# Ten quads instead of eight, a second lane for the state-space constants, the sink as a score column, and another division of PSUM

## The chip, the core and the metric

The kernel runs on one core of a Trainium2 chip. The core has five engines with queues of their own: TensorE (PE, its weight loads shown as PEld), VectorE (DVE), ScalarE (ACT), GpSimd (POOL) and SyncE (SP, here only a queue that issues DMAs). Work is measured in device microseconds for one execution; lower is better. A profile of one execution shows every instruction with its engine, its line of the kernel and its tile.

## What is computed

One step of a hybrid decoder layer for two groups of tokens that share all weights: 16 meta tokens and 512 prompt tokens, and 8 sample tokens with caches. Of the reference, what matters here:

```python
xn = rmsnorm(x, norm_gain)
h = einsum('btd,de->bte', xn, w_in)              # 2048 -> 8704
q, k, v, z_a, u, z_s, g_a, g_s = split(h)
q, k = rope(rmsnorm(q, gq)), rope(rmsnorm(k, gk))
# sliding window of 128 with 16 meta keys and a sink per head
m = maximum(max(s), sink); p = exp(s - m)
w = p / (sum(p) + exp(sink - m)); o = w @ v
# state space: 64 groups of 64 complex states, one linear recurrence over time
lam_bar = exp(lam * dt); b_bar = (lam_bar - 1) / lam * b
h_t = lam_bar * h_{t-1} + b_bar u_t;  y = real(c h) + d u
y = gelu(y); y = y * sigmoid(y @ w_glu + b_glu)
out = x + (sigmoid(g_a) * ((o * silu(z_a)) @ w_attn_out) + sigmoid(g_s) * ((y * silu(z_s)) @ w_ssm_out)) @ w_out
```

Everything is float32. The large products run as three matmuls of a faster float32 format each: both operands are split into a high and a low part (hi·hi, lo·hi, hi·lo).

## The kernel before, in words

The 536 tokens lie in two halves of 268 columns. A weight **unit** is 1024 rows by 128 columns; `Stream.piece` (L825) loads it (`raw`, a DMA on SP's queue), ACT casts the high part (`whi`, L829) and DVE subtracts for the low part (`wlo`, L830). A **block** of 128 output columns, `mm` (L938), takes two units: 16 k-tiles, three products, two halves. `xblock` (L969) makes a block of the gates and z parts and `evac` (L977) writes it to DRAM (`gD`).

A **quad** (`quad`, L1124, with `Quads`, L847) makes two blocks at once by seven products of half size each instead of eight (Strassen's scheme): `product` (L1117) issues 8 x 3 matmuls for each, from weights that are partly sums made by DVE (L887) and split like the others (L888, L889), and from sums of the inputs (`tau`, L1168). `NA` (L768) plain blocks run first while the tau are made, then `NQ` quads. Eight more quads do the last matrix, `w_out`.

The order of PE: five blocks beside the loading of x; four plain blocks; eight quads; then 27 blocks in the order of `ORDER1` (L771): 7 x blocks, 12 heads blocks (q, k, v; raw to `rawD`), 8 u blocks; then the remaining x blocks up to 47 (L1336); one block that is split around the reading of the state-space output (L1341); 8 blocks of `w_glu` with one unit each (L1363), 16 of `w_ssm_out` (L1379), 16 of `w_attn_out` on A (L1398) and the last quads.

Beside this runs **background** work, written as generators in the two lanes of `Background` (L777). After every 24 main matmuls `mm` calls `bg.step` with half a budget (`BUDGET`, `BUDGET2` and so on, L762 and 763); a generator yields its cost in us or `None`, which ends its lane's turn; the credit left over is cut to 0.5. In lane 0 come first the tau, then `ssm_prep` (L67), then for each u block `ssm`: `ssm_consts` (L235), the constants of that block, and `ssm_block` (L326), the recurrence: U is read back from DRAM, B·U on PE (L357), two scans on DVE (L386), C·H on PE (L406, L408), gelu. Then `attention` (L1268): ten loads of constants, `keys` (L498), `values` (L524, transposes L540), and for each of four key heads `queries` (L547) and four `blocks` (L634): `scores` (L561, 8 matmuls into two PSUM buffers, read by ACT L576 and DVE L578), `softmax` (L581), `turn` (transposes, L604) and `weigh` (L623). After the first key head `sample` (L668) starts in lane 1: it streams the sample's cache through DVE with DMAs on POOL's queue, and ends at L757. When both lanes are empty, `attended` (L1307) multiplies the result by the gate, read back by POOL (`zr`, L1322), and splits it into A (L1304, L1305). In attention each background instruction is ordered behind the last weight split on DVE.

The framework orders each engine's instructions by a timeline that it simulates when the program is built (`schedule_with_timeline_sim=True`, L1595), by priority and by when inputs and buffers come free there; on the chip each engine then works strictly in that order and waits where an input is later than planned. Weights and evacuations have a higher priority (`HIGH`).

PSUM has eight banks. Four belong to `mm` (two buffers of two banks) and four to `aux`, which serves all background products and the heads' sums: two buffers of two banks, one name.

## Time and profile before

| | |
|---|---|
| median of 3 runs | 1306.85 us (1305.33 to 1308.04) |
| profiled execution, its own time | 1305.66 us |
| its span | 1303.8 us |
| PE, DVE, ACT, POOL busy | 1287.2, 970.7, 529.2, 51.6 us |
| quads (115 to 271 us): PE, DVE, ACT busy of 156 us | 156.00, 122.60, 74.12 |
| state-space blocks (367 to 690): of 323 us | 322.50, 254.90, 82.43 |
| attention, first half (690 to 860): of 170 us | 164.23, 113.74, 89.78 |
| attention, second half (860 to 1047): of 187 us | 186.72, 134.13, 94.33 |
| mean granted clock of PE | 0.997 |

Busy times are sums over instructions of an engine; a matmul's shown duration overlaps the next one's, so the distance between matmuls is the measure of PE's pace and not their mean length. In a row of groups stand line, engine, operation, tiles, shape and count, then busy time and mean ns, then idle time before them and what ended it. In a row of waits stand the waiter, what it waited for, the total, how often, and the longest.

### The profile page before, as it was taken

How to read it: one execution, taken by the hardware profiler on the slowest of the kernel's cores; microseconds unless marked ns; L12 is line 12 of the kernel's file. 1: busy time of each engine (PE TensorE's matmuls, PEld its weight loads, DVE VectorE, ACT ScalarE, POOL GpSimd, SP SyncE). 2: the span in 40 equal slices, each digit the busy share in tenths (PEclk: the TensorE clock that was granted, in tenths of full speed). 3: DMA queues.
4: the chain of work that ended last, by engine and by line, in shares of the span. 5: the costliest groups of instructions: out<-in, count | busy, mean ns of one | idle time of the engine just before them, and what ended most of it. 6: DMA issues, size and time to landing. Idle time of an engine off the chain costs nothing.

```text
span 1303.8 us, 26285 instructions
## 1 busy us (share of the span) xinstructions
PE 1287.2 (99%) x10525; PEld 1250.8 (96%) x10525; DVE 970.7 (74%) x1723; ACT 529.2 (41%) x988; POOL 51.6 (4%) x115
## 2 busy tenths in 40 slices
PE   9999999999999999999999899999999999999998
PEld 8999999999999999999999899989998999999998
DVE  7586887768799788777963865878766677888775
ACT  8553444432222222222222567556544333344442
POOL 0000000000000000000004002111001100000000
PEclk9999999999999999999999899999999999999999
DMA  9554344243466554455447752666465865554441
GB/s 293 191 171 147 106 140 161 74 151 116 142 176 179 146 144 147 136 151 139 127 145 181 208 156 86 179 234 198 149 208 185 282 218 179 179 176 150 146 146 50
DMA packets 114010, 211.64 MB, mean 162 GB/s; under 512 B 29356, under 2 KB 54044, under 8 KB 113856
## 3 DMA queue, kind: packets, MB, share of 16 engines
q1 hardware_dynamic: 109216, 196.07, 48.3%
q0 software_dynamic: 4672, 13.89, 3.7%
q8 instruction: 83, 1.36, 0.4%
q14 instruction: 39, 0.32, 0.1%
HBM read 178.87 MB, written 33.13 MB: 163 GB/s over the span
## 4 chain that ended last, share of the span: by engine, by line
PE 82%; DMA 7%; issue 4%; DVE 2%; ACT 2%; SPq 1%; POOL 1%; POOLq 0%; DVEq 0%; ACTq 0%
PE mm L949 49%; PE pr L1120 23%; PE aux L628 2%; PE aux L1120 1%; DMA zr<-gD 1%; PE aux L357 1%; PE aux L408 1%; PE aux L949 1%; PE mm L1034 1%; DMA t<-gD 1%; PE aux L406 1%; PE aux L1100 1%; DVE wlo L830 1%; DMA uD<-uf 1%; DMA k_kg<-in_kg 1%
## 5 line engine op out<-in xcount | busy, mean ns | idle before, releaser
L949 PE MATMUL mm<-xh,whi 128*128 128x260 f32 (+1 forms) x1504 | 312.4, 288 | 0.0
L949 PE MATMUL mm<-xh,wlo 128*128 128x260 f32 (+1 forms) x1504 | 308.0, 285 | 0.0
L949 PE MATMUL mm<-xl,whi 128*128 128x260 f32 (+1 forms) x1504 | 306.7, 285 | 0.0
L829 ACT CAST whi<-raw 128x1024 fp32r<-128x1024 f32 (+3 forms) x156 | 152.2, 982 | 306.7 <-PE mm L949 234.3
L949 PEld LDWEIGHTS mm<-xh,whi 128*128 128x128 f32 x1504 | 233.9, 189 | 7.7 <-issue 7.6
L949 PEld LDWEIGHTS mm<-xl,whi 128*128 128x128 f32 x1504 | 234.6, 189 | 0.8 <-issue 0.8
L949 PEld LDWEIGHTS mm<-xh,wlo 128*128 128x128 f32 x1504 | 233.6, 189 | 1.6 <-issue 1.6
L830 DVE TENSOR_TENSOR wlo<-raw,whi 128x1024 fp32r<-128x1024 f32 (+3 forms) x156 | 176.5, 1137 | 65.7 <-ACT whi L829 64.1
L889 DVE TENSOR_TENSOR wlo<-raw,whi 128x1024 fp32r<-128x1024 f32 x112 | 134.5, 1222 | 48.7 <-ACT whi L888 48.2
L888 ACT CAST whi<-raw 128x1024 fp32r<-128x1024 f32 x112 | 115.6, 1049 | 120.5 <-PE pr L1120 40.9
L1120 PE MATMUL pr<-cb,whi 128*128 128x260 f32 x848 | 153.1, 283 | 2.4 <-ACT whi L888 2.4
L1120 PEld LDWEIGHTS pr<-cb,whi 128*128 128x128 f32 x848 | 130.8, 188 | 2.8 <-ACT whi L888 2.8
L949 PE MATMUL mm<-Y,whi 128*128 128x260 f32 x768 | 129.1, 286 | 0.3 <-DVE Y L1305 0.2
L1120 PE MATMUL pr<-cb,wlo 128*128 128x260 f32 x424 | 118.9, 283 | 0.0
L949 PEld LDWEIGHTS mm<-Y,whi 128*128 128x128 f32 x768 | 106.7, 188 | 6.4 <-issue 5.8
L1120 PE MATMUL pr<-tau,whi 128*128 128x260 f32 x480 | 86.6, 283 | 0.0
L949 PE MATMUL mm<-A,whi 128*128 128x260 f32 x512 | 82.5, 283 | 0.0
L1120 PEld LDWEIGHTS pr<-cb,wlo 128*128 128x128 f32 x424 | 79.6, 188 | 0.0
L949 PE MATMUL mm<-Y,wlo 128*128 128x260 f32 x384 | 79.2, 286 | 0.0
L887 DVE TENSOR_TENSOR raw<-raw 128x1024 f32<-128x1024 f32 x64 | 78.2, 1222 | 1.3
L1120 PEld LDWEIGHTS pr<-tau,whi 128*128 128x128 f32 x480 | 73.7, 188 | 0.0
L949 PEld LDWEIGHTS mm<-A,whi 128*128 128x128 f32 x512 | 70.3, 188 | 0.3 <-DVE A L1305 0.3
(415 smaller groups left out, 2026.3 us busy)
## 6 DMA issues: line engine op xcount, KB each, us to landing
raw<-in_w SPq DMA_DIRECT2D x202, 512.0 KB, 3.8
gD<-z SPq DMA_DIRECT2D x48, 260.0 KB, 2.7
t<-gD SPq DMA_DIRECT2D x32, 260.0 KB, 2.8
cache<-in_vc POOLq DMA_DIRECT2D x16, 286.0 KB, 3.5
cache<-in_kc POOLq DMA_DIRECT2D x15, 288.0 KB, 3.5
xr<-in_x SPq DMA_DIRECT2D x16, 268.0 KB, 5.6
xg<-in_x SPq DMA_DIRECT2D x8, 536.0 KB, 5.4
sD<-z SPq DMA_DIRECT2D x16, 260.0 KB, 2.7
```

The source lines that it names most:

```text
L357: nc.tensor.matmul(bu[:, i, 140 * e:140 * e + 140], lhsT=D["B"][:, i, 2 * h + e], rhs=U[:, 2 * h + e, 8:16 + NC], start=True, stop=True)
L406: nc.tensor.matmul(o, lhsT=R["T"][:, a], rhs=U[:, a, 0:140], start=True, stop=False)
L408: nc.tensor.matmul(o, lhsT=D["CL"][:, a, i, 1:5], rhs=H[:, a, i, 0:140], start=False, stop=(i == 1))
L628: nc.tensor.matmul(pv[64 * e:64 * e + 64, 0, 0:256], lhsT=V, rhs=pr[:, e::2], start=(i == 0), stop=(i == len(parts) - 1))
L829: nc.scalar.copy(out=hi, in_=raw)
L830: self.dve = nc.vector.tensor_tensor(out=lo, in0=raw, in1=hi.bitcast(F32), op=ALU.subtract).ins
L887: nc.vector.tensor_tensor(out=o, in0=o, in1=i, op=ALU.add)
L888: nc.scalar.copy(out=hi, in_=t)
L889: nc.vector.tensor_tensor(out=lo, in0=t, in1=hi.bitcast(F32), op=ALU.subtract)
L949: m = nc.tensor.matmul(ps[:, c, 0:W], lhsT=wt[:, k], rhs=xo(kt, c), start=f, stop=l)
L1034: nc.tensor.matmul(ps[:, c, 0:260], lhsT=wt[:, kt % 8], rhs=xo[:, kt, c, 8:CH], start=f, stop=l)
L1120: m = nc.tensor.matmul(bank, lhsT=wt[:, p], rhs=x(p, e), start=first and f and p == 0, stop=l and p == 7, skip_group_check=not first and l ...
```

## The change

`NQ` goes from 8 to 10, so 20 of the x blocks are made by quads and 11 in place of 15 are left for the end of the loop; `XORDER` puts the blocks 32 to 39 ahead of 24 to 31. In `ssm_prep` all small normalisations but one go. The constants of the eight state-space blocks become one generator in lane 1, with double buffers, up to two sets ahead; their products with a per-partition factor go from DVE to ACT (`times`). The U of a block is loaded as soon as its buffer is free. `Background` keeps up to 3 (later 2) of credit, serves the lanes in turn until attention and lane 0 first from then on; budgets and some costs are new. In attention the constants come with one load, the values' and keys' loads are issued first, the values come before the keys, the sample starts at once, the second half of each key tile is copied by a DMA on POOL's queue, and the sink becomes a 145th score column, written by POOL, so that maximum and sum include it. The four background banks become one pair (`aux`) and two single banks (`tr`, `wg`); during the state-space blocks these are held as fixed regions. The `w_glu` blocks' tanh goes to SBUF instead of in place in PSUM. The diff, cut to its core:

```diff
     for n in ("z2", "z4"):
         nz = tmp.tile([P, 2, 32], F32, name=n)
         cmul(nc, tmp, nz, z, z[:, 0], z[:, 1], (32,), "c32_")
-        norm(nz, (32,), "n32")
         z = nz
     zs = yield from powers(T6, z, 6, "za")
     Z = tmp.tile([P, 2, 32], F32, name="Z")
     cmul(nc, tmp, Z, zs[2], zs[1][:, 0], zs[1][:, 1], (32,), "c32_")
-    norm(Z, (32,), "n32")
...
     cmul(nc, tmp, c, Zs[3], Zs[1][:, 0], Zs[1][:, 1], (32,), "c32_")
     cmul(nc, tmp, c2, c, Z[:, 0], Z[:, 1], (32,), "c32_")
+    norm(c2, (32,), "n32")
...
+def ssm_consts(nc, pool, dram, R, D, ub, a_bT, a_bN, a_cT, e32, d_skip, later, free):
...
+    bN = pool.tile([P, 4, 2, 32], F32, name="bN", bufs=1)
+    nc.sync.dma_start(out=bN, in_=a_bN[:, ps])
+    c = pool.tile([P, 4, 2, 32], F32, name="c", bufs=1)
...
+    yield 0.0
+    yield None
...
+
+    def times(dst, src, x):
+        nc.scalar.activation(out=dst, in_=src, func=AF.Copy, scale=x)
+
+    for a in range(4):
+        q = slice(4 * ub + a, 4 * ub + a + 1)
+        for i, k in enumerate(("Fre", "nFre")):
+            times(s1[:, a, i], bN[:, a, i], R[k][:, q])
+        times(s2[:, a], bN[:, a], R["nFim"][:, q])
+    yield 0.0
+    yield None
+    for r, t in ((0, t1), (1, t2)):
+        for k in range(4):
+            for a in range(4):
+                times(t[:, a, :, k], c[:, a], R["lamp"][:, r, k, 4 * ub + a:4 * ub + a + 1])
+            if k % 2:
+                yield 0.0
+                yield None
+    while not free():
+        yield None
+    B = pool.tile([P, 2, 512], F32, name="B")
     nc.sync.dma_start(out=B, in_=a_bT[ub])
...
-    v.tensor_tensor(out=t1, in0=B, in1=bc(f4[:, 0], 1, 2), op=ALU.mult)
-    v.tensor_tensor(out=t2, in0=B, in1=bc(f4[:, 1], 1, 2), op=ALU.mult)
-    yield 2.4
...
-            v.tensor_tensor(out=t[:, :, i], in0=bc(c[:, :, i], 2, 4), in1=bc(lp, 3, 32), op=ALU.mult)
-        yield 1.4
+    yield 3.8
+    v.tensor_tensor(out=bb[:, :, 0], in0=s1[:, :, 0], in1=s2[:, :, 1], op=ALU.add)
+    v.tensor_tensor(out=bb[:, :, 1], in0=s1[:, :, 1], in1=s2[:, :, 0], op=ALU.add)
+    yield 0.6
...
-    s1 = pool.tile([P, 4, 2, 32], F32, name="s1", bufs=1)
-    s2 = pool.tile([P, 4, 2, 32], F32, name="s2", bufs=1)
-    bb = pool.tile([P, 4, 2, 32], F32, name="bb", bufs=1)
...
+    kp = R["kp"]
+    with later():
+        for a in range(4):
+            for i in range(2):
...
-    d0 = pool.tile([P, 8, L], F32, name="d0", bufs=1)
+    d0 = R["d0"][ub % 2]
...
     tab = D["tab"]
...
+    with later():
+        for h in range(2):
+            for e in range(2):
+                for i in range(2):
+                    nc.tensor.matmul(place(h, i, e), lhsT=D["B"][:, i, 2 * h + e], rhs=U[:, 2 * h + e, 8:16 + NC],
+                                     start=True, stop=True)
+    yield 0.0
+    yield None
...
     with later():
-        y = psum.tile([P, 2, 512], F32, name="aux")
...
-                for part in (slice(0, 64), slice(64, 128)):
-                    for dst, src in zip(tm(KH, part), (*T, M)):
-                        nc.scalar.copy(out=dst, in_=src)
-                for part in (slice(0, 64), slice(64, 128)):
-                    for dst, src, hi in zip(tm(KL, part), (*T, M), tm(KH, own)):
-                        v.tensor_tensor(out=dst, in0=src, in1=hi.bitcast(F32), op=ALU.subtract)
-                    yield 0.8
+                for dst, src in zip(tm(KH, own), (*T, M)):
+                    nc.scalar.copy(out=dst, in_=src)
+                for dst, src, hi in zip(tm(KL, own), (*T, M), tm(KH, own)):
+                    v.tensor_tensor(out=dst, in0=src, in1=hi.bitcast(F32), op=ALU.subtract)
+                other = slice(64 - 64 * h, 128 - 64 * h)
+                for K in (KH, KL):
+                    nc.gpsimd.dma_start(out=K[other], in_=K[own])
+                yield 1.0
...
-        sb = pool.tile([P, 2, CH], F32, name="sb")
+        sb = pool.tile([P, 2, CH], F32, name="sv")
...
-        vb = pool.tile([P, 4, P], F32, name="vb", tag="rb")
+        vb = pool.tile([P, 4, P], F32, name="vb", tag=("po", "pp")[e], bufs=1)
...
-            ps = self.psum.tile([P, 2, 512], F32, name="aux")
+            ps, pm = (self.psum.tile([P, 512], F32, name=n) for n in ("tr", "wg"))
             for b in range(4):
-                nc.tensor.transpose(out=ps[:, 0, 128 * b:128 * b + 128], in_=vb[:, b], identity=self.C["idn"])
...
-        S = pool.tile([P, 4, 144], F32, name="S")
+        S = pool.tile([P, 4, 145], F32, name="S")
+        nc.gpsimd.tensor_copy(out=S[:, :, 144], in_=C["sink"][:, 4 * kv:4 * kv + 4])
         for j in range(2):
...
-        sk = C["sink"][:, 4 * kv:4 * kv + 4]
         v.tensor_reduce(out=m, in_=S, axis=AX.X, op=ALU.max)
-        v.scalar_tensor_tensor(out=m, in0=m, scalar=0.125, in1=sk, op0=ALU.mult, op1=ALU.max)
-        nm = pool.tile([P, 4], F32, name="nm")
-        v.tensor_scalar(out=nm, in0=m, scalar1=-1.0, scalar2=None, op0=ALU.mult)
+        v.tensor_scalar(out=m, in0=m, scalar1=-0.125, scalar2=None, op0=ALU.mult)
         den = pool.tile([P, 4], F32, name="den")
         for r in range(4):
-            nc.scalar.activation(out=S[:, r], in_=S[:, r], func=AF.Exp, bias=nm[:, r:r + 1], scale=0.125,
+            nc.scalar.activation(out=S[:, r], in_=S[:, r], func=AF.Exp, bias=m[:, r:r + 1], scale=0.125,
                                  accum_out=den[:, r:r + 1])
-        v.tensor_tensor(out=m, in0=sk, in1=m, op=ALU.subtract)
-        nc.scalar.activation(out=nm, in_=m, func=AF.Exp)
-        v.tensor_tensor(out=den, in0=den, in1=nm, op=ALU.add)
...
-        ps = self.psum.tile([P, 2, 512], F32, name="aux")
+        ps, pv = (self.psum.tile([P, 512], F32, name=n) for n in ("tr", "wg"))
...
-        pv = self.psum.tile([P, 2, 512], F32, name="aux")
...
             self.P = self.softmax(kv, S)
-            yield 2.0
+            yield 1.2
...
-BUDGET = 5.0
-BUDGET2, BUDGET3, BUDGET4 = 4.4, 2.4, 3.6
+BUDGET = 5.8
+BUDGET2, BUDGET3, BUDGET4 = 4.6, 2.4, 3.8
...
-NA, NQ = 4, 8
-
-XORDER = list(range(16, 24)) + list(range(16)) + list(range(24, 48))
+NA, NQ = 4, 10
+
+XORDER = list(range(16, 24)) + list(range(16)) + list(range(32, 40)) + list(range(24, 32)) + list(range(40, 48))
...
     def step(self, budget):
-        self.credit = min(self.credit, 0.5) + budget
-        for q in self.lanes:
-            while q and self.credit > 0:
+        self.credit = min(self.credit, self.cap) + budget
+        ways = list(self.lanes)
+        while any(ways) and self.credit > 0:
+            for q in ways if self.fair else ways[:1]:
+                if not q or self.credit <= 0:
+                    continue
                 try:
                     with ExitStack() as st:
...
                 if cost is None:
+                    ways = [w for w in ways if w is not q]
                     break
                 self.credit -= cost
+            ways = [w for w in ways if w]
...
     def drain(self):
         while any(self.lanes):
-            for q in self.lanes:
-                for cost in q.pop(0) if q else ():
-                    self.credit -= cost or 0.0
+            self.step(1e6)
+        self.credit = 0.0
 
...
-    auxc, mmc = (tc.tile_pool(name=n, bufs=2, space=PS) for n in ("auxp", "mmp"))
+    auxc, mmc = (tc.tile_pool(name=n, bufs=b, space=PS) for n, b in (("auxp", 1), ("mmp", 2)))
...
+    S, sp, Ds = {}, None, {}
+    ready, done, uDs = -1, 0, {}
+
+    def ssm_sets():
+
+        nonlocal ready
+        for ub in range(8):
+            Ds[ub] = {}
+            yield from ssm_consts(nc, sp, dram, S, Ds[ub], ub, A["bT"], A["bN"], A["cT"], e32, dsk,
+                                  lambda: tc.issue_after(bg.last), lambda: ub - 2 not in Ds)
+            ready = ub
+
+    def load_u():
+
+        for ub in sorted(uDs):
+            if ub < done + 2:
+                ssm_load(nc, S["U"][ub % 2], uDs.pop(ub))
+
+    def ssm(ub):
+        nonlocal done
+        while ready < ub:
+            yield None
+        yield from ssm_block(nc, sp, S, Ds[ub], ub, yD[ub], lambda: tc.issue_after(bg.last))
+        del Ds[ub]
+        done = ub + 1
+        load_u()
...
-            ps = aux.tile([P, 2, 512], F32, name="aux")
+            if "ax" not in S:
+                S["ax"] = aux.tile([P, 2, 512], F32, name="aux")
+            ps = S["ax"][:, 1, P:]
...
-            S["T"] = sp.tile([P, 4, P], F32, name="T", bufs=1)
-            S["U"] = sp.tile([P, 4, 16 + NC], F32, name="U", bufs=1)
...
+            S["T"] = [sp.tile([P, 4, P], F32, name="T") for _ in range(2)]
+            S["U"] = [sp.tile([P, 4, 16 + NC], F32, name="U") for _ in range(2)]
...
+            S["H"] = sp.tile([P, 4, 2, 9 + NC], F32, name="H", bufs=1)
+            S["d0"] = [sp.tile([P, 8, L], F32, name="d0") for _ in range(2)]
...
+            S["bu"] = [aux.tile([P, 512], F32, name=n) for n in ("tr", "wg")] + [S["ax"][:, 0]]
+            S["kp"] = S["ax"][:, 1, 0:P]
+            bg.add(ssm_sets(), lane=1)
...
-        bg.add(ssm(n, flat(uf)))
+        uD = dram.tile([P, 2 * CH], F32, name="uD", bufs=8)
+        nc.sync.dma_start(out=uD, in_=flat(uf))
+        uDs[n] = uD
+        load_u()
+        bg.add(ssm(n))
...
-        for nm in ("cos", "sin", "kg", "kgs", "qg", "qgs", "mown", "bd64", "sink"):
-            C[nm] = const(nm, ap, bufs=1)
-        C["mprev"] = const("mprev", ap, I32, bufs=1)
+        attc = const("attc", ap, bufs=1)
+        C["cos"], C["sin"] = (attc[:, CH * 2 * n:CH * 2 * n + 2 * CH].rearrange("p (c w) -> p c w", c=2) for n in range(2))
...
-        yield 0.0
-        yield from at.keys(O["k"])
-        for e in range(2):
-            yield from at.values(e)
+        vals = [at.values(e) for e in range(2)]
+        keys = at.keys(O["k"])
+        for g in (*vals, keys):
+            next(g)
+        bg.add(at.sample(A["ssk"], A["kc"], A["vc"]), lane=1)
+        yield None
+        for g in vals:
+            yield from g
+        yield from keys
         at.load_q(0)
         yield None
         for kv in range(4):
             yield from at.queries(kv)
             yield from at.blocks(kv, kv == 3)
-            if kv == 0:
-                bg.add(at.sample(A["ssk"], A["kc"], A["vc"]), lane=1)
-
-
+
+
+    bg.fair, bg.cap = False, 2.0
```

230 lines of the change are left out of this document (118 added, 112 removed).

## The prediction

> **What bounds the kernel now.** I read first the busy shares at the top of the page, then PE's part of the waits, then the busy time by stage, and last the chain of waits to the end.
>
> ```profile
> span 1303.8 us, 26285 instructions
> PE 1287.2 (99%) x10525; PEld 1250.8 (96%) x10525; DVE 970.7 (74%) x1723; ACT 529.2 (41%) x988; POOL 51.6 (4%) x115
> PE aux L540 <- DVE vb L531: 5.4, 1, 5.4
> PE pr L1120 <- ACT whi L888: 2.4, 2, 1.3
> ...
> PE aux L572 <- DVE QT L557: 0.3, 2, 0.2
> 115.00:271.00 156.00, 156.00 (x1301) 156.00 (x1300) 122.60 (x123) 74.12 (x101) 0.00 (x0) 1.00 0.38 127
> 367.00:690.00 323.00, 322.50 (x2720) 315.49 (x2719) 254.90 (x510) 82.43 (x134) 1.60 (x14) 1.00 0.51 149
> ```
>
> PE is busy 1287.2 of 1303.8 us: time can only be won by giving PE fewer matmuls or by filling its few gaps, and work of DVE, ACT or POOL that is saved off PE's path is worth nothing by itself. The waits (total, times, longest) hold one gap of size, 5.4 us before line 540. Two stages, the quads (115 to 271) and the state-space blocks (367 to 690), have no gap worth the name; the large one lies behind them, where attention begins.
>
> The profiled execution took 1305.66 us, span and 1.86 us around it, and the median of the runs is 1306.85. I do the sum against 1305.66 and add the 1.2 us of difference at the end.
>
> **The change part by part.** (1) *Two more quads.* What is a matmul worth? From the chain of waits (start, length, engine and line, count):
>
> ```profile
> 56.33 58.64 PE mm L949 x486
> 138.99 131.66 PE pr L1120 x1096
> ```
>
> A plain block issues one matmul per 58.64/486 = 0.121 us, a quad one per 131.66/1096 = 0.120 us. Two plain blocks are 2 x 16 k-tiles x 3 products x 2 halves = 192 matmuls; a quad does the same two blocks in 7 x 8 x 3 = 168. Ten quads for eight save 2 x 24 = 48 matmuls: 48 x 0.120 = **5.8 us**, and all of it lies on PE's path. What it adds elsewhere:
>
> ```profile
> L889 DVE TENSOR_TENSOR wlo<-raw,whi 128x1024 fp32r<-128x1024 f32 x112 | 134.5, 1222 | 48.7 <-ACT whi L888 48.2
> L887 DVE TENSOR_TENSOR raw<-raw 128x1024 f32<-128x1024 f32 x64 | 78.2, 1222 | 1.3
> ```
>
> A quad needs 7 splits and 4 sums where two blocks need 4 splits: 7 more DVE operations, 8.6 us at 1.222. DVE was busy 122.60 of 156 us in that stage while PE lost nothing, and each further quad brings the same mix, so I cost this at nothing. Without the cover it would be DVE's excess over 20 us per quad, and there is none. But the two quads also push everything behind them back by 2 x 168 x 0.120 = 40.3 us, and take four plain blocks (46 us) away from the end of the loop beside which attention runs; that is rival C.
>
> (2) *The gap before the values' transposes.* The timeline of PE:
>
> ```profile
> 723.96 0.40 PE L949 MATMUL mm<-xh,whi 128*128 128x260 f32 x2
> 729.80 1.11 PE L540 MATMUL aux<-k_idn,vb 128*128 128x128 f32 x4 [5.45 <-DVE vb L531]
> 730.71 0.42 PE L541 MATMUL aux<-k_idn,mt 128*64 128x128 f32 x1
> 730.78 0.78 PE L949 MATMUL mm<-xl,whi 128*128 128x260 f32 x2
> ...
> 735.26 0.54 PE L949 MATMUL mm<-xh,wlo 128*128 128x260 f32 x2
> 735.64 0.40 PE L949 MATMUL mm<-xh,whi 128*128 128x260 f32 x2
> 730.00:735.00 5.00, 5.00 (x24) 4.96 (x24) 4.01 (x11) 1.75 (x7) 0.00 (x0) 0.50 0.54 153
> ```
>
> The price is more than the 5.45 us. From 729.80 to 735.64 PE does five transposes and 22 main matmuls (11 rows of two). The second such group of transposes takes about 0.5 us at full clock, 22 matmuls take 2.6, so 5.8 us go for 3.1: another 2.7 us, at a granted clock of 0.50. In all **8.1 us**. [...]
>
> Why was vb late? DVE's order held the keys' rope in front of it, and that waited for loads:
>
> ```profile
> 705.15 0.78 DVE L482 SCALAR_TENSOR_TENSOR sb<-sb,k_kg,k_cos 128x536 f32<-128x536 f32 x1 [5.58 <-DMA sb<-rawD]
> 711.23 0.78 DVE L483 SCALAR_TENSOR_TENSOR sw<-sw,k_kgs,k_sin 128x536 f32<-128x536 f32 x1 [3.57 <-DMA rb<-rkD]
> 728.79 0.29 DVE L531 COPY vb<-sb 128x256 f32<-128x256 f32 x1
> k_kg<-in_kg SPq DMA_DIRECT2D x1, 0.5 KB, 7.2
> sb<-rawD SPq DMA_DIRECT2D x4, 268.0 KB, 2.8
> ```
>
> After the change the values' loads are first on SP's queue, ten loads of constants become one, and the values come ahead of the keys. What is late next is that load itself: 2.8 us at the median, 5.58 us of wait in the worst row. Kept 0, lost 8.1 are the ends; I take 6 us as gone, near the lower of the two waits.
>
> (3) *State-space constants.* DVE loses these (count, busy, mean ns):
>
> ```profile
> L268 DVE TENSOR_TENSOR rt<-c,lamp 128x512 f32<-128x512 f32 x32 | 20.0, 682 | 0.0
> L280 DVE TENSOR_TENSOR s<-bN,nF 128x256 f32<-128x256 f32 x8 | 3.3, 416 | 0.0
> L171 DVE TENSOR_TENSOR n32a<-n32a 128x32 f32<-128x32 f32 x9 | 1.7, 190 | 0.2
> L600 ACT ACTIVATE Pn<-S,den 128x128 f32<-128x128 f32 x64 | 20.5, 392 | 3.8 <-DVE den L596 3.7
> L399 ACT ACTIVATE pst<-H x16: 195/209/211, 392.5 to 678.1; 128x4 f32<-128x4 f32 x16
> SPq L243 <- DVE rt L250: 13.8, 6, 2.7
> ```
>
> 20.0 + 3.3 and two smaller products go, some 28 us in eight sets, and eight of nine small norms, four operations of about 0.2 us each, 6.5 us. ACT takes them over in 44 instructions per set, 352 in all, of 32 or 64 columns with a scale per partition. No row has that shape: above it 0.392 us (128 columns, such a scale), below it 0.209 (4 columns): 74 to 138 us; at 0.34, nearer L600, 120. ACT was busy 82.43 of 323 us there, so it goes to about 62%, and I cost it at nothing on PE: weights are cast two units (11.5 us) ahead, and a burst of eight such instructions takes 2.7. A set's loads (six of them, on SP's queue among the weights) move one set ahead; today they wait up to 2.7 us there for a buffer, with weight loads behind them, and PE did not feel it. The sets as a lane of their own cost PE the same matmuls.
>
> (4) *Softmax, keys, cost numbers.* Three operations of four columns per block go from DVE, one from ACT; half of the keys' copies become DMAs. The POOL queue gets 8 of these and 16 copies of the sink column. Behind each stands the loading of the sample's cache, which itself waited for DVE; whoever is late there delays a reduction on DVE, not PE directly. Nothing on PE's path, worth only what it does for C.
>
> (5) *PSUM.* Two pairs of banks become one pair and two single ones. New is a wait: the second pair of score matmuls waits until the first has been read.
>
> ```profile
> L576 ACT COPY S<-aux 128x288 f32<-128x288 f32 x32 | 12.4, 396 | 15.0 <-PE aux L573 14.9
> L578 DVE COPY_PREDICATED S<-k_mprev,aux 128x256 f32<-128x256 int32 x24 | 10.6, 446 | 15.9 <-ACT S L576 15.7
> 744.20 0.29 PE L573 MATMUL aux<-KL,QT 128*128 128x272 f32 x1
> 744.32 0.40 PE L949 MATMUL mm<-xh,whi 128*128 128x260 f32 x2
> ```
>
> The order of PE is planned from simulated times, and it puts main matmuls between the parts of a group, as at 744.32, until the buffer is due. With that cover the wait costs nothing but lateness of chip against plan. Its lower end is 0 (it takes no matmul away, so no gain), its upper end is D. I take 0.1 us for each of 16 blocks, the size of the two short waits on QT in the list: 1.5 us.
>
> Sum: -5.8 - 6 + 1.5 = -10.3. 1305.66 - 10.3 = 1295.4, and 1.2 for the median: **1296.6**.
>
> **The rivals.** *B: the gap stays or moves.* The values' transposes, or another group behind a load (the sample's first DVE operations now come at the start, behind 14 POOL loads), wait as long as before. For: the DMA waits above, 5.58 and 3.57 us, and DVE works in order. Against: the values are now ahead. Then the 6 us are not won: 1296.6 + 6 = 1302.6, from 1300 to 1305.
>
> *C: attention comes too late, slower.* The place is the first matmul on A.
>
> ```profile
> L1266 DVE TENSOR_TENSOR uf<-mm,R x8: 703/708/717, 350.8 to 637.7; 128x536 f32<-128x536 f32 x8
> 661.89 0.43 DVE L365 TENSOR_TENSOR p<-aux,tab 128x264 f32<-128x264 f32 x1 [1.73 <-PE aux L357]
> 1021.40 0.54 ACT L757 COPY oT<-aux 64x32 f32<-64x32 f32 x4 [2.14 <-PE aux L752]
> 1047.04 0.62 DVE A L1305
> 1047.71 2.30 PE mm L949 x17
> ```
>
> There is no slack today: A is split at 1047.67 and PE starts on it at 1047.71. State-space work ends at 678.1 (pst), the sample at 1021.9, 343.8 us later; then 25.8 us of loads and splits follow until A. After the change the last u comes 40.3 us later (678); without the set's constants in the way, the block needs about 26 us in place of 40 (two DMAs and their waits, some 10, then 661.89 to 678.1), so attention starts near 704. A is due at 1047.7 - 11.8 = 1036, the sample at 1010: 306 us, 11% less than 343.8. The costs that the code gives to the lanes fall from 151.6 to 136.4, and the budget rises from 4.4 to 4.6: 343.8 x 0.90 x 0.957 = 296. Ten us to spare, and more if the credit that was thrown away above 0.5 is now used. The point that decides is a shortening of 11%; from there each us late is a us lost. With half of that, 19 us late and 2.7 for the slowed clock: 1296.6 + 22 = 1318; from 1301 to 1320.
>
> *D: the single PSUM pair.* If PE stands for each second pair, 0.396 + 0.446 = 0.84 us, or 2.06 with one 1.22 us split ahead on DVE: 16 times, 13 to 33 us, less the 1.5 counted: 1308 to 1328. For: every block has it. Against: today four users per block share two buffers as tightly, and no PE wait on an evacuation is in the list. [...]
>
> **How the numbers follow.** Forecast, 1290 to 1300: 0.57. B 0.18, C 0.15, D 0.10. Range 1289 to 1309: the lower end is the whole 8.1 us gone and 4 us of finer packing, the upper takes in B and the mild part of C and D; out are 0.03 below, 0.07 of C and 0.08 of D. A measurement tells about 0.2% from no change, 2.6 us. Faster (under 1304.2): 0.57, 0.15 of B, 0.03 of C: 0.75. Within: 0.03 of B, 0.04 of C, 0.01 of D: 0.08. Slower: 0.17.
>
> **What would show it.** PE records fall by 48; the quad stage is 40 us longer with no wait on whi; no wait before the values' transposes and no clock under 1.00 behind it; ACT busy about 120 us more and DVE some 30 less between quads and attention; PE's waits still under 3 us in all there. Wrong: a wait of PE on A (C), many short ones on S (D), or on a kp or H (part 3, ACT behind its plan).

## The result and the profile after

The changed kernel takes 1309.93 us (median of 20 runs, 1303.76 to 1313.94) against 1305.55 us of the kernel before on the same chips. The ratio is 1.0028, 95% interval 1.0018 to 1.0038: slower by 0.28%. The forecast was 1296.6 us, 0.8% faster than the 1306.85 us it started from; it is 13.3 us off, and the time lies just above its range.

The top of the page of the kernel after, and PE's part of its waits (total, times, longest):

```profile
span 1308.3 us, 26441 instructions
PE 1275.5 (97%) x10477; PEld 1247.4 (95%) x10477; DVE 950.6 (73%) x1651; ACT 611.0 (47%) x1329; POOL 63.7 (5%) x133
```

```profile
PE aux L721 <- DVE qs L715: 7.8, 1, 7.8
PE mm L981 <- ACT A L1383: 2.9, 1, 2.9
PE tr L379 <- DMA U<-uD: 2.5, 2, 1.6
PE tr L434 <- DVE H L422: 2.5, 2, 1.2
...
PE mm L981 <- DVE uf L1331: 2.0, 1, 2.0
PE mm L981 <- ACT Y L1383: 1.8, 1, 1.8
PE pr L1177 <- ACT z L1189: 1.1, 2, 0.8
...
PE tr L573 <- issue: 0.9, 1, 0.9
```

PE has 48 matmuls fewer, as forecast, and is busy 11.7 us less. But it stands still for 1308.3 - 1275.5 = 32.8 us, before 16.6. So 16.2 us of new standing eat the 11.7 and leave 4.5 us, which is the difference of the two spans. The values' transposes wait 0.9 us in place of 5.4 (line 573, 540 before), and in their place the sample's transposes wait 7.8 (line 721).

Where the time went, by stage: the distances from one matmul's start to the next one's on PE were added up, less each matmul at the usual distance of its form (the smaller of the two kernels' medians). What is left is waiting, slow clock and the cost of short groups, in us. The last three columns are kernels of the experiments: the sample started later, the same with eight quads, and the fastest kernel of all. Each column is one execution. How much counts as usual depends on how forms are told apart, so only the differences between columns are to be read; told apart in another way, those of the stages between before and after stay within about half a us.

| stage of PE | before | after | later sample | later sample, 8 quads | fastest |
|---|---|---|---|---|---|
| matmuls at usual distance | 1257.9 | 1250.7 | 1251.5 | 1257.6 | 1251.4 |
| start | 7.0 | 7.8 | 7.4 | 7.2 | 9.3 |
| quads | -0.7 | 1.4 | 1.3 | -0.5 | 1.6 |
| constants' preparation | -0.8 | -1.2 | -1.3 | -1.0 | -1.6 |
| state-space blocks | 2.1 | 9.6 | 9.8 | 4.2 | 6.4 |
| to the first scores | 9.1 | 13.2 | 9.5 | 7.1 | 7.1 |
| first scores to A | 20.3 | 13.5 | 9.4 | 12.0 | 10.3 |
| from A on | 2.2 | 7.2 | 2.7 | 1.1 | 3.1 |

(Of the 7.2 us between the first two columns of the first row, 5.8 are the 48 matmuls, which is exactly the difference of the records, 10525 and 10477. The other 1.4 us are an error of this bookkeeping.) The quads lose 2 us, the state-space blocks 7.5, the start of attention 4, the part from A on 5; attention between first scores and A wins 7.

**The gap.** PE's timeline in the kernel after (start, length; in brackets the wait before it):

```profile
770.11 0.28 PE L981 MATMUL mm<-xl,whi 128*128 128x260 f32 x1
778.15 0.42 PE L721 MATMUL aux<-k_idn,qs 128*64 128x128 f32 x1 [7.76 <-DVE qs L715]
...
783.57 0.64 PE L981 MATMUL mm<-xl,whi 128*128 128x260 f32 x2
784.00 0.45 PE L981 MATMUL mm<-xh,wlo 128*128 128x260 f32 x2
784.29 0.40 PE L981 MATMUL mm<-xh,whi 128*128 128x260 f32 x2
784.53 0.40 PE L981 MATMUL mm<-xl,whi 128*128 128x260 f32 x2
```

Until 784 two matmuls start every 0.43 us, then every 0.24: as before, the gap is followed by 6 us at half clock (granted clock 0.50 from 778 to 784 us). What made qs late stands in DVE's timeline:

```profile
763.51 0.30 DVE L712 TENSOR_SCALAR qs<-x,k_attc 128x64 f32<-128x64 f32 x1
...
769.31 0.76 DVE L515 SCALAR_TENSOR_TENSOR sw<-sw,k_attc 128x520 f32<-128x520 f32 x1 [5.21 <-DMA t<-yD]
...
773.40 0.21 DVE L714 TENSOR_TENSOR qs<-qs,s 128x64 f32<-128x64 f32 x1
...
777.20 0.76 DVE L515 SCALAR_TENSOR_TENSOR sw<-sw,k_attc 128x520 f32<-128x520 f32 x1 [1.30 <-issue]
777.88 0.21 DVE L715 TENSOR_TENSOR qs<-qs,r 128x64 f32<-128x64 f32 x1
```

The sample's own loads are there: its first operation, at 763.51, waits for nothing. But between the sample's four steps (lines 712 to 715) DVE's order holds the rope of the first query tiles (line 515, 520 columns), and that waits 5.21 us for its loads. (The row names a load of y as the last to land; the operation reads sw.) Rival B named this group of matmuls, but another cause. It is not the sample's loads on POOL's queue that are late; it is the queries' loads, for which another operation waits ahead of the sample's on DVE.

**The state-space blocks.** ACT and DVE in the kernel after:

```profile
499.35 7.77 ACT L256 ACTIVATE ct<-c,lamp 128x64 f32<-128x64 f32 x32 [4.42 <-DMA c<-in_cT]
507.02 1.03 ACT L861 CAST whi<-raw 128x1024 fp32r<-128x1024 f32 x1
```

```profile
508.09 1.23 DVE L862 TENSOR_TENSOR wlo<-raw,whi 128x1024 fp32r<-128x1024 f32 x1 [3.69 <-ACT whi L861]
509.23 0.43 DVE L422 TENSOR_TENSOR H<-rt,rt 128x264 f32<-128x264 f32 x1
```

A chain of four queues: ACT stands 4.42 us before the load of c and then runs 32 products in one go, 7.77 us. The weights' cast stands behind them, DVE's split behind the cast (3.69 us of waiting), H behind the split, and PE's C·H behind H (the row of waits on H above: 2.5 us in two). The weights were in time, as forecast; what stood behind the split on DVE was not.

**A.** The first block on A, PE and then ACT:

```profile
1053.23 1.54 PE L981 MATMUL mm<-A,whi 128*128 128x260 f32 x6 [2.88 <-ACT A L1383]
```

```profile
1052.56 0.62 ACT L1383 CAST A<-oT 128x520 fp32r<-128x520 f32 x1 [4.84 <-DVE oT L1403]
```

```profile
L1331 DVE TENSOR_TENSOR uf<-mm,R x8: 689/707/718, 392.3 to 688.8; 128x536 f32<-128x536 f32 x8
L426 ACT ACTIVATE pst<-H x16: 193/209/211, 435.3 to 724.7; 128x4 f32<-128x4 f32 x16
```

The last u comes at 688.8, 51.1 us later than before and not 40.3, because the state-space stage is itself longer; its work ends at 724.7, not near 704. So attention has less time than forecast, and A comes 3 us late.

### The profile page after: what moved, and what is told of

Read it like the earlier page. It is cut to its first block, busy times and chain, and to the rows that moved or that the text cites. A ratio compares the mean times of both kernels' runs of the same rounds, so it can differ in the third digit from the quotient of the medians.

```text
span 1308.3 us, 26441 instructions
## 1 busy us (share of the span) xinstructions
PE 1275.5 (97%) x10477; PEld 1247.4 (95%) x10477; DVE 950.6 (73%) x1651; ACT 611.0 (47%) x1329; POOL 63.7 (5%) x133
## 4 chain that ended last, share of the span: by engine, by line
PE 73%; DMA 11%; DVE 7%; ACT 5%; issue 2%; SPq 1%; POOL 0%; ACTq 0%; DVEq 0%; POOLq 0%
PE mm L981 39%; PE pr L1177 25%; ACT ct L256 2%; PE wg L654 2%; DMA xr<-in_x 2%; DMA sw<-rawD 2%; DVE wlo L862 2%; PE aux L1177 1%; DMA zr<-gD 1%; DMA gD<-z 1%; DMA xg<-in_x 1%; PE aux L981 1%; PE aux L605 1%; PE aux L606 1%; PE mm L1433 1%
## 5 line engine op out<-in xcount | busy, mean ns | idle before, releaser
L981 PE MATMUL mm<-xh,whi 128*128 128x260 f32 (+1 forms) x1376 | 284.2, 287 | 2.9 <-DVE uf L1331 2.0
L981 PE MATMUL mm<-xl,whi 128*128 128x260 f32 (+1 forms) x1376 | 283.5, 286 | 0.0
L981 PE MATMUL mm<-xh,wlo 128*128 128x260 f32 (+1 forms) x1376 | 281.9, 285 | 0.0
L981 PEld LDWEIGHTS mm<-xh,whi 128*128 128x128 f32 x1376 | 214.4, 189 | 5.8 <-issue 2.6
L981 PEld LDWEIGHTS mm<-xl,whi 128*128 128x128 f32 x1376 | 215.7, 189 | 2.1 <-issue 2.0
L981 PEld LDWEIGHTS mm<-xh,wlo 128*128 128x128 f32 x1376 | 213.7, 189 | 1.6 <-issue 1.6
L921 DVE TENSOR_TENSOR wlo<-raw,whi 128x1024 fp32r<-128x1024 f32 x126 | 151.3, 1223 | 57.5 <-ACT whi L920 54.2
L1177 PE MATMUL pr<-tau,whi 128*128 128x260 f32 x608 | 110.0, 283 | 0.0
L1177 PEld LDWEIGHTS pr<-tau,whi 128*128 128x128 f32 x608 | 93.5, 188 | 0.0
L1177 PE MATMUL pr<-tau,wlo 128*128 128x260 f32 x304 | 85.0, 283 | 0.0
```

The source lines that it names most:

```text
L921: nc.vector.tensor_tensor(out=lo, in0=t, in1=hi.bitcast(F32), op=ALU.subtract)
L981: m = nc.tensor.matmul(ps[:, c, 0:W], lhsT=wt[:, k], rhs=xo(kt, c), start=f, stop=l)
L1177: m = nc.tensor.matmul(bank, lhsT=wt[:, p], rhs=x(p, e), start=first and f and p == 0, stop=l and p == 7, skip_group_check=not first and l ...
```

## The experiments

All edits are to the changed kernel unless "before" is named. Times are medians; ratios are to the kernel before.

**First four: which part does what.** Eight quads:

```diff
-NA, NQ = 4, 10
+NA, NQ = 4, 8
```

> The changed kernel with eight quads in place of ten, all else as changed. Theory (the quads' matmuls are won in full, the loss lies in waits of the attention stage that do not come from the quads): 48 matmuls more at 0.120 us, so 1309.9 + 5.8 = about 1315.7 us, and PE still waits about 3 us for A. Rival (the two quads shorten the window for attention, and A is late for that reason): the wait for A (3.2 us) and the slow clock behind it (about 1.7 us) go, so 1309.9 + 5.8 - 4.9 = about 1310.8 us, with no PE wait on A.

1305.77 us, ratio 1.0006 (0.9993 to 1.0020). Neither: with 48 matmuls more the kernel is 4.2 us faster by the medians, though the two intervals overlap a little. The wait for A goes, as the rival said, and the state-space stage and the quads lose less as well.

The sample started after the first key head, as before the change:

```diff
-        bg.add(at.sample(A["ssk"], A["kc"], A["vc"]), lane=1)
...
             yield from at.blocks(kv, kv == 3)
+            if kv == 0:
+                bg.add(at.sample(A["ssk"], A["kc"], A["vc"]), lane=1)
```

> The changed kernel with the sample started where it was before the change, after the first key head. Theory (PE's 7.8 us gap is the sample's transposes, whose DVE operations stand between the first query's rope operations, which wait for loads): the gap and the slow clock behind it, about 11 us, go: about 1299 us with no PE wait on qs. Rival (the early start is what lets attention end in time): the sample ends later, the wait for A grows from 3 us by more than 8, and the time stays at 1307 to 1320 us.

1296.93 us, ratio 0.9929 (0.9909 to 0.9949), 13 us faster than the changed kernel. In its waits:

```profile
PE aux L605 <- DVE QT L589: 5.2, 1, 5.2
...
PE tr L434 <- DVE H L422: 2.2, 2, 1.2
PE mm L981 <- DVE uf L1331: 2.2, 1, 2.2
PE tr L379 <- DMA U<-uD: 2.1, 2, 1.1
...
PE mm L981 <- ACT A L1384: 0.4, 1, 0.4
```

The wait on qs is gone and A is nearly in time: the early start was not needed, it made attention later. But a gap of 5.2 us remains, now before the first scores, which need the same queries. That the time is the forecast one, 1296.6 us, is chance: the gap and the losses in the state-space stage, which the forecast did not have, are still there.

Ten quads alone on the kernel before:

```diff
-NA, NQ = 4, 8
+NA, NQ = 4, 10
```

> The kernel before with ten quads in place of eight, nothing else changed. If the quads are worth their matmuls wherever they stand: 1305.6 - 5.8 = 1299.8 us. If the background work of the kernel before has no slack (A was split 0.04 us before PE began on it): state-space work and attention start 40 us later and have 46 us less until A is due, so PE stands before A for 20 to 46 us: 1320 to 1346 us.

1326.74 us, ratio 1.0161 (1.0144 to 1.0178): the second case. It is rival C in full size. Its waits, besides 6.5 us before the values:

```profile
PE mm L949 <- ACT A L1304: 5.4, 2, 5.2
PE aux L628 <- DVE po L613: 5.0, 3, 2.7
```

The end of attention runs without main matmuls between its parts; from 1020 to 1060 us the granted clock is 0.83 and then 0.59. So the rest of the change does bring room for two more quads, but not quite enough.

The values ahead of the keys, alone, on the kernel before:

```diff
-        yield from at.keys(O["k"])
         for e in range(2):
             yield from at.values(e)
+        yield from at.keys(O["k"])
```

> The kernel before with the values ahead of the keys in attention, nothing else changed. Theory (the gap before the values' transposes comes from the keys' rope standing ahead of them on DVE): the 5.4 us gap and the 2.7 us of slow clock behind it go: about 1297.5 us. Rival (the gap only moves, to the first scores or another group behind a load): 1303 to 1306 us, with a PE wait of 3 us or more at another line within 30 us.

1304.96 us, ratio 0.9995 (0.9983 to 1.0007): the rival. The waits say it in two lines:

```profile
PE aux L572 <- DVE QT L557: 5.2, 1, 5.2
PE aux L540 <- DVE vb L531: 2.8, 2, 1.5
```

The 5.4 us before the values have become 5.2 before the first scores. The order of values and keys is worth nothing by itself.

**The remaining gap and the waits in the state-space stage.** All with the later sample. More time between a set's loads and ScalarE's products:

```diff
     nc.sync.dma_start(out=c, in_=a_cT[:, ps])
     yield 0.0
-    yield None
+    for _ in range(4):
+        yield None
```

> The changed kernel with the later sample, and four turns in place of one (11.5 us for 2.9) between the loads of a set's c and bN and their use on ScalarE. Theory (ScalarE stands 17.0 us before c in the state-space stage, weights queue behind it, and PE's 6.5 us of small waits there on H, U and uf come from this): ScalarE's waits on c go, and PE's waits between 390 and 690 us fall from 6.5 to under 2: 1297 - 5 = about 1292 us. Rival (these waits come from the shared PSUM regions and the DVE chain, not from ScalarE): ScalarE's waits go and PE's stay, 1297 us within 1.5.

1357.98 us, ratio 1.0403. Both missed the main thing. PE's waits on H and U do fall (1.0 us on H is left, and 3.4 us on another tile are new), but each set takes three turns more, and the stage's last instruction is at 775.4 in place of 724.7 us. Attention is that much too late, and PE stands in one piece for the sample's last group:

```profile
L427 ACT ACTIVATE pst<-H x16: 193/209/212, 443.6 to 775.4; 128x4 f32<-128x4 f32 x16
```

```profile
PE aux L780 <- DVE o_s L776: 16.8, 1, 16.8
```

The gap before the first scores is 9.3 us. Together, 50.7 us of lateness cost 61 us: in this kernel a late state-space stage is paid for in full.

The first queries' quarter loads on POOL's queue:

```diff
-            nc.sync.dma_start(out=sw[32 * q:32 * q + 32], ...)
+            (q0 or nc.sync).dma_start(out=sw[32 * q:32 * q + 32], ...)
```

> The changed kernel with the later sample, and the eight quarter loads (sw) of the first two query tiles issued on POOL's queue in place of SP's. Theory (the gap at the start of attention is the first queries' rope waiting for loads that come late through SP's queue, 7 issues of about 0.55 us per tile among weights): the 5.2 us gap before the first scores and about 2.5 us of slow clock go: about 1290 us. Rival (the loads wait for buffers that the keys still use, whatever queue they stand in): the gap stays at 4 to 6 us, 1296 to 1298 us.

1298.21 us, ratio 0.9946 (0.9926 to 0.9965): the gap is 3.4 us in two pieces, the time the same as without. Not decided.

The first scores held back by three turns:

```diff
             yield from at.queries(kv)
+            for _ in range(0 if kv else 3):
+                yield None
```

> The changed kernel with the later sample, and the first scores held back by three turns of the background (72 main matmuls, 8.6 us) behind the first queries. Theory (PE's order puts the first scores where the plan has QT ready, and the chip has it 5.2 us later; main matmuls in between would cover that): the 5.2 us gap and its slow clock go, 1297 - 7.5 = about 1289.5 us, if attention keeps 8.6 us to spare. Rival (attention has no slack left, PE already waits 0.4 us for A): the wait for A grows to 3 to 9 us and the time is 1293 to 1300 us.

1305.36 us, ratio 0.9998 (0.9986 to 1.0010): the rival, and worse. The gap falls to 2.9 us, the wait for A grows to 4.0 in three pieces, and 8.4 us are lost. The slack behind attention is less than the 8.6 us of delay.

Eight quads with the later sample (the edit of the first run):

> The changed kernel with the later sample and eight quads in place of ten. With eight quads and the early sample the time was 1305.8, 4 us better than ten. If the quads are worth their 48 matmuls as soon as attention ends in time: 1297 + 5.8 = about 1302.7 us. If the two quads cost as much elsewhere as they save (more small waits in the state-space stage): 1296 to 1299 us.

1295.97 us, ratio 0.9931 (0.9914 to 0.9948): nearest the second case, within 1 us of ten. The table shows where the two quads lose what they save: 1.8 us in the quads and 5.6 in the state-space blocks.

The products back on DVE, as seven broadcast operations for each set:

```diff
-        for i, k in enumerate(("Fre", "nFre")):
-            times(s1[:, a, i], bN[:, a, i], R[k][:, q])
-        times(s2[:, a], bN[:, a], R["nFim"][:, q])
+    for i, k in enumerate(("Fre", "nFre")):
+        v.tensor_tensor(out=s1[:, :, i], in0=bN[:, :, i], in1=bc(R[k][:, ps], 2, 32), op=ALU.mult)
...
-                times(t[:, a, :, k], c[:, a], R["lamp"][:, r, k, 4 * ub + a:4 * ub + a + 1])
+            v.tensor_tensor(out=t[:, :, i], in0=bc(c[:, :, i], 2, 4), in1=bc(lp, 3, 32), op=ALU.mult)
```

> The changed kernel with the later sample and ten quads, and the per-partition products of the state-space constants back on DVE (7 operations per set in place of 44 on ScalarE), the lane, the loads and the PSUM regions kept. Theory (the new small waits of PE in the state-space stage, 6.5 us on H, U and uf, come from ScalarE's bursts of these products and its standing before c, with weight casts behind): they fall to under 2 us and the time from 1297 to about 1292 us. Rival (they come from the lane, the loads of U or the PSUM regions; or the 28 us that DVE gets back weigh more): PE's waits there stay at 4 us or more, 1296 to 1302 us.

1299.01 us, ratio 0.9950 (0.9937 to 0.9963). PE's waits in the stage, 385 to 690 us:

```profile
PE tr L376 <- DMA U<-uD: 2.3, 2, 1.6
PE mm L978 <- DVE t L467: 1.8, 1, 1.8
```

The waits on H and uf are gone, so ScalarE's products have a part in them. They are not all of it: with eight quads and the products still on ScalarE, the waits on H and uf are 0.7 and 0.8 us in place of 2.2 each. The waits on U stay and do not come from the products, and one on t of 1.8 us is new, so PE's waits in the stage fall from 6.5 to 4.1 us. The median does not show even that. The execution that was profiled took 1294.13 us, the fastest of six, with a gap of 6.0 us before the first scores; what the slower ones waited for is not on record.

A swapped copy of the raw heads in DRAM, so that attention loads a tile by four transfers in place of seven:

```diff
-        for q in range(4):
-            b = 32 * (q ^ 1)
-            nc.sync.dma_start(out=sw[32 * q:32 * q + 32], in_=self.raw[i][b:b + 32, :, cs])
+        nc.sync.dma_start(out=sw, in_=self.swp[i][:, :, cs])
```

> The changed kernel with the later sample and ten quads, and a swapped copy of the raw keys and queries written to DRAM when the heads are made, so that each tile of attention is loaded by four transfers in place of seven (48 transfers less there, 40 more in the heads' blocks). Theory (PE's 5.2 us gap before the first scores is the lateness of loads that SP's queue issues one after the other): the gap goes, 1297 - 7 = about 1290 us. Rival (the loads wait for the buffers of the keys, or the order of DVE, not for SP): the gap stays at 4 us or more, 1295 to 1299 us.

1298.57 us, ratio 0.9955 (0.9939 to 0.9971): the gap is 6.2 us. The number of SP's issues is not what holds the queries.

The same with eight quads:

> As the run with the swapped copy, with eight quads in place of ten. With seven transfers eight and ten quads took the same time (1296.0 and 1296.9 us). If the two quads' matmuls are eaten by waits whose size hangs on how the stages fall, about the same again: within 3 us of the run with ten. If they are worth their 5.8 us once the gap is gone: 5 to 6 us slower than it.

1296.06 us, ratio 0.9924 (0.9912 to 0.9937): eight quads again no slower than ten.

**Are the DMA engines full?** In the windows of the later sample's kernel (DMA share and GB/s at the end) they look so:

```profile
730.00:740.00 10.00, 10.00 (x86) 10.00 (x85) 4.55 (x7) 2.36 (x3) 1.80 (x4) 1.00 0.43 124
...
760.00:770.00 10.00, 10.00 (x85) 10.00 (x85) 5.63 (x12) 2.00 (x6) 1.27 (x3) 1.00 1.14 283
770.00:780.00 10.00, 6.83 (x57) 6.62 (x55) 5.45 (x10) 2.51 (x5) 1.82 (x4) 1.00 1.09 253
```

Four kernels took bytes away or added some. The key halves by ScalarE and DVE:

```diff
-                for K in (KH, KL):
-                    nc.gpsimd.dma_start(out=K[other], in_=K[own])
+                for part in (slice(0, 64), slice(64, 128)):
+                    for dst, src in zip(tm(KH, part), (*T, M)):
+                        nc.scalar.copy(out=dst, in_=src)
...
```

> The changed kernel with the later sample and ten quads, and the second halves of the key tiles made by ScalarE and DVE again, in place of eight copies of 144 KB by DMA. Theory (at the start of attention the DMA engines are full: share 1.0 to 1.15 from 740 to 780 us, 0.45 before; every byte less there brings the first queries sooner): 1.15 MB less of some 10.5 MB, about 4.6 us of DMA time at 250 GB/s, so the gap before the first scores falls from 5.2 to about 1 to 3 us and the time to 1292 to 1294 us, less what 24 more small operations cost. Rival (the order of DVE sets the gap, not the DMA engines): gap 5 us or more, 1297 us or more.

1294.62 us, ratio 0.9912 (0.9898 to 0.9926): 2 us faster by the medians, with intervals that overlap; the gap is 4.2 us in two pieces.

```diff
+        dum = dram.tile([4, P, 2, CH], F32, name="dum")
+        for n in range(4):
+            nc.gpsimd.dma_start(out=dum[n], in_=rawD[n])
```

> The changed kernel with the later sample and ten quads, and four more transfers of 268 KB that nothing needs (raw heads copied to a spare buffer), issued from POOL's queue at the start of attention. Theory (DMA engines full there): 1.07 MB read and written more, 4 to 9 us of their time, so the gap before the first scores grows from 5.2 to 9 us or more and the time by 4 to 10 us, 1301 to 1307 us. Rival (order of DVE): the gap stays at 5 to 6 us, 1296 to 1298 us.

1296.03 us, ratio 0.9926 (0.9910 to 0.9942): no slower, and the gap is 3.2 us. So the gap did not grow with the bytes, and my theory of full DMA engines falls in this form. (Each gap here is that of one execution, and the executions of this kernel lie 6.2 us apart, those of the later sample's 7.4, so a difference of 2 us between two gaps says little.)

The sample's loads tied behind the first softmax by copies of one of its results:

```diff
+        for t in (x, sw, rb):
+            self.hold(t.rearrange("p a b -> p (a b)"))
...
+            if c < 2:
+                self.hold(t[:, 0, 0:1])
```

> The changed kernel with the later sample and ten quads, and the sample's 18 small loads and its first two cache loads (0.73 MB) tied behind the first softmax by small copies on POOL; until now they went out at the start of attention although the sample is started later. Theory (DMA engines full): 0.73 MB and some 1500 small packets less in that window, so the gap before the first scores falls from 5.2 to under 3 us, and the time to 1291 to 1294 us if the sample still ends in time. Rival (order of DVE, or the sample now ends late): gap 5 us, or a wait for A that grows by more than 3 us: 1297 us or more.

1304.70 us, ratio 0.9993 (0.9983 to 1.0002): the rival. The gap is 6.2 us and A is 2.8 us late again.

Both reliefs together, with eight quads:

> Eight quads, later sample, the sample's loads behind the first softmax, and the key halves by ScalarE and DVE: both reliefs of the DMA engines together. Theory (DMA engines full): the gap before the first scores (4.4 us with eight quads) goes almost whole, no clock under 1.00 there: 1296 - 5 = about 1291 us. Rival: 1295 us or more.

1299.85 us, ratio 0.9952 (0.9937 to 0.9966): the rival. The gap is only 2.3 us with no copies and no early sample loads, but the kernel is 3.9 us slower than the later sample with eight quads; what is lost lies behind the first scores.

**The best of it.** The key halves by the engines, with eight quads:

> Later sample, key halves by ScalarE and DVE, and eight quads. With ten quads this kernel took 1294.6 us. In three pairs so far ten quads were 4.1, 0.9 and 2.5 us slower than eight, although they save 5.8 us of matmuls. If that holds (the matmuls are eaten by lateness in the state-space stage and attention): 1291 to 1295 us. If the quads are worth their matmuls once the start of attention is lighter: about 1300 us.

1298.45 us, ratio 0.9937 (0.9923 to 0.9951): here eight quads are 3.8 us slower than ten by the medians.

The key halves by the engines, with ten quads and the products on DVE:

> Later sample, key halves by ScalarE and DVE, ten quads, and the products of the state-space constants back on DVE. If ScalarE's bursts cause the waits on H and uf in the state-space stage (4.4 us together with ten quads): these go, 1294.6 - 3 = about 1291.5 us. If DVE's 28 us more weigh as much: 1294 to 1298 us.

1292.94 us, ratio 0.9892 (0.9873 to 0.9912): the fastest, 1.1% under the kernel before. As in the other kernel with the products on DVE, no wait on H or uf is left in its state-space stage; PE waits there 3.4 us on U and 1.4 us on t.

## Why the prediction was wrong

**The step that failed** is the gap: "Kept 0, lost 8.1 are the ends; I take 6 us as gone." The mechanism behind it was half right: DVE's order and late loads. The values did come in time. But the price of the gap was counted as won, though the same lateness stood ready for the next group. In the kernel before with the values first that group is the first scores (5.2 us), in the changed kernel the sample's transposes (7.8), with the later sample the first scores again (5.2). The load that is late next was put at 2.8 us at the median and 5.58 in the worst row. On the way to the first scores single loads take 7 to 10 us (rows at the end of this section), and in the kernel before three loads at the start of attention already took 6.6 to 7.2 us. The start of attention did not get 6 us cheaper but 4.1 dearer (9.1 to 13.2). Rival B had the right group, but its price, 6 us not won, is that of a gap that keeps its size; a gap that moves can also grow.

Within that step stands the sample. The prediction says that its operations now come at the start, and puts no cost of its own on it. Started later, the same kernel is 13.0 us faster with ten quads and 9.8 us with eight. The first is about the whole difference between forecast and result, so this one part decides the sign.

**The second step** is a cost set at nothing: "I cost it at nothing on PE", of the constants on ACT. The instruction is cheaper than priced, 0.243 us each (7.77 / 32) against 0.34, and ACT is busy 81.8 us more against 120. I looked for the cover in the wrong place. The weights, two units ahead, were in time; H stood behind their split on DVE. The prediction had named a wait on H as a sign of being wrong, and it came. The state-space stage lost 7.5 us. Of these 4.5 are the waits on H and uf, which went when the products did (and shrank with eight quads too), and 2.5 the waits on U, which did not go with the products. A set's loads, which "move one set ahead", are late by 17.0 us in four waits:

```profile
ACT ct L256 <- DMA c<-in_cT: 17.0, 4, 4.5
```

**The quads**: 48 matmuls fewer was right, but "I cost this at nothing", of what they add, was not. In four pairs of kernels that differ in nothing else, ten quads against eight gave +4.2, +1.0, +2.5 and -3.8 us, on average 1 us slower where 5.8 faster was forecast. Part of it lies in the quads themselves. All twelve kernels with ten quads show a wait of 0.7 to 1.5 us on the reading of a quad's bank (line 1189 here), and none of the seven with eight does. ACT, which reads the bank, waits there for a store:

```profile
272.00 0.67 ACT L1189 ACTIVATE z<-pr 128x260 f32<-128x260 f32 x2 [2.32 <-DMA gD<-z]
```

The larger part, in the pair that the table shows, lies in the state-space blocks. The two quads put everything behind them 41 us later; why PE then waits more in that stage was not taken apart, and the fourth pair went the other way.

**Rival C** was right in its place and mild in its size: A is 2.9 us late, and PE then runs at half clock for 3.4 us (granted clock 0.51 from 1053.7 to 1057.1 us), which costs about 1.7 more. My 10 us of slack rested on 704 us for the start of attention: the last u at 678 and 26 us behind it. The last u came at 688.8 and the state-space work ended 35.9 us behind it, at 724.7. With three turns of delay there was no slack at all. How much this decides is shown by ten quads on the old kernel (+21 us) and by the constants made late (+61).

**Rival D** did not come: no wait on S of any size is in the list, and the 1.5 us taken for it were not spent. On the other side I missed that attention got cheaper: 20.3 to 13.5 us between the first scores and A. Most of it is the weighing matmuls: from the start of each to the start of the next, 176 of them take 28.3 us before and 22.6 after. I did not follow why.

By stages the sum is: -7.2 in the first row (5.8 of it matmuls), +2.5 start, quads and preparation, +7.5 state-space, +4.1 start of attention, -6.8 attention, +5.0 from A on: +5.1, against 4.5 us of the spans.

**What stays open** is what would make the first queries come in time; with the later sample PE waits 2 to 9 us for them in every kernel. It is not the number of SP's issues, and not the bytes alone. The chain of waits shows what it is made of. In the later sample's kernel, between 740 and 779 us, four loads stand one behind another in it (start, and length from issue to landing):

```profile
740.17 10.13 DMA sb<-rawD
750.76 7.02 DMA sb<-rawD
759.69 7.38 DMA sw<-rawD
771.17 6.94 DMA rb<-rqD
```

These are 31.5 of 38 us, and operations on the keys stand between the later ones. Keys and queries share two buffers of each tile, and SP's longest wait from 735 to 785 us is the load of a query tile waiting until the keys have been written out:

```profile
SPq L496 <- DMA out_k<-sb: 3.8, 2, 2.9
```

No run gave the queries buffers of their own, so that this is the cause is not shown.

## What to carry to other kernels

A wait that one group of matmuls showed belonged here to the queue that was late, not to the group (5.4 us before the values' transposes became 5.2 before the first scores): before counting such a wait as won, ask which group needs the same queue next, and price the gap there. Work moved to an idle engine that also feeds the bound engine was not free (352 products on ACT, 4.5 us of PE's waits on H and uf): follow every queue behind it to the end, two engines further. Where PE is 99% busy and the background has no slack, a saving that pushes the background back can be worth less than its matmuls (two more quads: 1 us lost on average over four pairs, where 5.8 won were forecast), and only its own run says how much.

## What the runs showed of the hardware

In the kernel with the later sample the clock halved behind a wait of 1.91 us. PE's timeline around it, and the clock in the window behind it:

```profile
753.14 0.27 PE L574 MATMUL wg<-k_idn,mt 128*64 128x128 f32 x1 [1.91 <-DVE mt L567]
...
754.33 0.56 PE L981 MATMUL mm<-xh,whi 128*128 128x260 f32 x2
...
757.72 0.47 PE L981 MATMUL mm<-xh,wlo 128*128 128x260 f32 x2
```

```profile
754.00:757.00 3.00, 3.00 (x18) 3.00 (x17) 2.09 (x4) 1.27 (x5) 2.09 (x5) 0.57 1.13 203
```

PE works for 1.2 us at full speed, then for 3.4 us at half (two matmuls start every 0.43 us in place of 0.24), which costs 1.7 us more. A wait of 1.76 us (Y, at 923 us of the changed kernel) had the same behind it (granted clock 0.52 from 924.2 to 927.6 us), one of 2.05 us (uf, at 689) had not (1.00 from 689 to 694 us). So waits of nearly the same length ended differently, and the price of one could not be read from its length; what decided it is not shown.
